# Weight halves, earlier casts, two stores on another queue, one difference moved: four small moves in a two-layer decoder trunk

## The chip, the cores and the metric

One core of one Trainium2 chip runs the whole program. It has five engines with a queue each: PE (matmuls), DVE (elementwise on vectors), ACT (activations and casts), POOL (GpSimd: masks, biases, and DMAs that add while they write) and SP (SyncE: it only issues DMAs). The engines run side by side, and each takes its own instructions strictly in the order of its queue. The metric is the time of one execution in device microseconds (us). The kernel before takes 1109.95 us, the median of three runs from 1109.84 to 1110.57.

## The reference, cut to what matters

The trunk has two layers over 512 positions of width 1024, in fp32. Layer 0 has a dilated attention with three groups of heads, layer 1 a forgetting attention with 16 heads of 64 on keys and values that are computed once; each is followed by a gated feed-forward net with a causal convolution.

```python
def fox_mixer(xn, w_q, w_o, k, v, c):
    q = (xn @ w_q).reshape(B, T, B_HEADS, HEAD_DIM)
    ...
        s = jnp.einsum('bqhd,bkhd->bhqk', q[:, q0:q1], k[:, :q1]) * scale
        s = s + (c_t[:, :, q0:q1, None] - c_t[:, :, None, :q1])
        s = jnp.where(causal, s, NEG)
        p = jax.nn.softmax(s, axis=-1)
        outs.append(jnp.einsum('bhqk,bkhd->bqhd', p, v[:, :q1]))
    ...
    return o.reshape(B, T, B_WIDTH) @ w_o

    # each layer: sandwich-normed mixer, then sandwich-normed feed-forward
    h = h + rms_norm(mix, g[1])
    f = conv_ffn(rms_norm(h, g[2]), w_up[l], conv_w[l], conv_b[l], w_down[l])
    h = h + rms_norm(f, g[3])
```

## The kernel before, in words

**Splitting.** Every fp32 operand of a large matmul is split into a high part (a cast to the shorter type fp32r, on ACT) and a low part (the original less the high part, on DVE). A product is then three matmuls on PE, one line each: high by high (L277), high by low (L278), low by high (L279). A weight of 128x1024 is loaded by SP into a buffer `wraw` (L49), cast by ACT (L57) and subtracted by DVE (L65). The class `W` keeps the order: `high` issues the next loads and the cast, `low` the subtraction. For the query weights of layer 1, `low_added` does the subtraction in a DMA instead: ACT writes the negated high part into the low part's place (L59), and a DMA of POOL adds `wraw` to it there (L82), so DVE has no part in it.

**Start.** Layer 0 begins with the projection of q and k (`qk_ps`). ACT and DVE norm a block of x (`sd`, `rs`, `xn`), PE transposes it (L345, `xt_ps`), ACT and DVE split the transposed block (L348, L349: `xah`, `xal`), and PE multiplies. The first weights come from `wearly`; those numbered 0, 1 and 2 are used by the first blocks, as soon as they are split.

**Forgetting attention.** It runs in steps m = 0 to 17; step m has a pair of heads j = m // 2 and two of the four blocks of queries (blocks 0 and 1 in even steps, 2 and 3 in odd ones). In a step stand, in this order: the scores (L1715, into four banks `s_ps`); the product of probabilities and values of step m-2 (L1762, into `o_ps`, from transposed probabilities `pT`); on DVE the score plus bias with its maximum (L1723), on ACT the exponential (L1725). Then, for each of the two blocks a = 0 and 1: the bias of step m+1 on POOL (L1696, with the causal mask L1697), a part of the next query projection (`q_ps`), the normalisation on DVE (L1733, L1735), the transposes of step m-1 on PE (L1747) and their copies on ACT (L1749); in late steps also a part of the output projection (`acc`) and the cast of an output weight. Every odd step ends with the high and low part of `o_ps` (L1772, L1776, `OTb`); every even step with the low part of the next queries (L1523, `qst`), which the scores two steps on multiply.

**Sums beside it.** Idle engines also prepare differences of blocks of the down projection's weights for the feed-forward net of layer 1. Loads bring them to `dsums`, DVE takes four differences of 128x512, and a store puts them into `dT` in memory, from where they are read much later. `down_sums` does this for two blocks (0 and 1) just ahead of the attention (`down1`; differences L607 to L610, two stores of 512 KB for each block, L615). `sums_between` does it for blocks 2 to 5 inside the attention: loads at the end of block a = 1 of step m = 2, 6, 10 and 14 (L1783 to L1785, on POOL), differences (L1787, L1788, L1790, L1791) in the two steps after it, then one store (L1793).

The order is written out by hand: generators are advanced by `next(...)` at given places. Buffers rotate in pools; `t4` holds biases, `ck` tiles (the rows of c of one pair of heads, loaded by SP, L1492) and `wraw` in turn, so a load can have to wait for the reader of an older tile.

Of the kernel before, what the change touches and what calls it, by code (L numbers as in the profile page):

```python
# [9 lines left out]
F32 = mybir.dt.float32  # L10
# [3 lines left out]
ALU = mybir.AluOpType  # L14
# [12 lines left out]

SEVEN = (5, 6, 8, 9, 11, 12, 14, 15, 17, 18)
ND = NF // 2
LAST = 3  # L30
FILL = 26


class Weights:
# [18 lines left out]
    def high(self, minus=False):  # L53
        if self.n_split < len(self.pieces):
            self.load(self.n_split + 1 + self.ahead_dma)
            raw, pair = self.raw.pop(self.n_split), self.new_pair()
            self.nc.scalar.copy(pair[:, 0], raw)  # L57
            if minus:
                self.nc.scalar.activation(pair[:, 1], raw, AF.Copy, scale=-1.0)  # L59
            self.half_done.append((raw, pair))  # L60

    def low(self):
        if self.half_done:
            raw, pair = self.half_done.pop()
            self.nc.vector.tensor_tensor(pair[:, 1], raw, pair[:, 0].bitcast(F32), ALU.subtract)  # L65
            if self.n_split in self.kept:
                self.kept[self.n_split] = raw
            self.ready[self.n_split] = (pair[:, 0], pair[:, 1])
            self.n_split += 1
# [32 lines left out]
def trunk_kernel(ctx, tc, x, norm_gains, w_qkv_a, w_o_a, w_q_b, w_o_b, kv_norm, w_kvf, b_f,  # L102
                 w_up, conv_w, conv_b, w_down, rope, out):
    nc = tc.nc
    act, dve, pool, pe, sp = nc.scalar, nc.vector, nc.gpsimd, nc.tensor, nc.sync
# [56 lines left out]

    dT = [tc.dram_tile([ND, 128, 2048], F32, name=f"dT{l}") for l in range(2)]

# [44 lines left out]
    W = Weights(nc, new_raw, lambda: t8([128, 2, 1024], F32R, name="w"), pieces)  # L209
# [382 lines left out]
    def down_sums(pairs, place, queue, lag, behind):  # L592


        live, n = [], len(pairs)
        for i in range(n + lag + behind):
            if i < n:
                l, j = pairs[i]
                a, b = place()
                live.append((a, b))  # L600
                r = w_down[l][j * 256:j * 256 + 256, :].rearrange("(c p) d -> c p d", p=128)
                sp.dma_start(a, r[0])
                sp.dma_start(b[:, 0:512], r[1, :, 512:1024])
                sp.dma_start(b[:, 512:1024], r[1, :, 0:512])
            if 0 <= i - lag < n:
                a, b = live[i - lag]
                dve.tensor_tensor(a[:, 0:512], a[:, 512:1024], a[:, 0:512], ALU.subtract)  # L607
                dve.tensor_tensor(a[:, 512:1024], b[:, 0:512], a[:, 512:1024], ALU.subtract)
                dve.tensor_tensor(b[:, 0:512], b[:, 0:512], a[:, 0:512], ALU.subtract)
                dve.tensor_tensor(b[:, 512:1024], b[:, 512:1024], b[:, 0:512], ALU.subtract)  # L610
            i -= lag + behind
            if i >= 0:
                l, j = pairs[i]
                for q, t in enumerate(live[i]):
                    queue.dma_start(dT[l][j, :, q * 1024:q * 1024 + 1024], t)  # L615
            yield

    def in_one():
# [13 lines left out]
    def ffn(l, bd, cp, nxt, ahead):  # L632
# [343 lines left out]
        for c in range(2, NF):  # L976
            if c == NF - 4:
                pair_load(0)
            if c == NF - 3:
                sums = down_sums([(l, ND - 1), (1, 8 + l)], in_one, pool, 1, 0)  # L980
                next(sums)
            if c in SEVEN:
                x21, x22 = [(xT[0][i], xT[1][i], s) for i, s in ((1, LO), (1, HI))]
# [311 lines left out]
    W.ahead = 4  # L1295
    W.split(6)
    qk_post(0, 3, qk_banks[3])
    sums = down_sums([(1, 6), (1, 7)], in_two, sp, 1, 3)
    next(sums)
    reorder(2, 3)  # L1300

# [23 lines left out]
        act.copy(V[1][:, b, :], o[:, 0:256])  # L1325
        dve.tensor_copy(V[2][:, b, :], o[:, 256:512])

    down0 = down_sums([(0, j) for j in range(10)], in_one, sp, 1, 1)
# [307 lines left out]
    for bp in range(2):  # L1636
        for s in range(2):
            t = slice(bp * 128, bp * 128 + 128)
# [13 lines left out]
                mm3(vc[bp], ah, al, w4[s][0][:, k, :], w4[s][1][:, k, :], False, False, True)  # L1652
        keep_values(0, bp, vc[bp])
    del w4
    down1 = down_sums([(1, j) for j in range(2)], in_two, pool, 1, 1)
    for c in range(4, 8):
        if c == 7:
            for i in range(4):
# [119 lines left out]
    def sums_between(l, j):  # L1778

        t = t8([128, 2, 1024], name="dsums")  # L1780
        a, b = t[:, 0], t[:, 1]
        r = w_down[l][j * 256:j * 256 + 256, :].rearrange("(c p) d -> c p d", p=128)
        pool.dma_start(a, r[0])  # L1783
# [3 lines left out]
        dve.tensor_tensor(a[:, 0:512], a[:, 512:1024], a[:, 0:512], ALU.subtract)  # L1787
        dve.tensor_tensor(a[:, 512:1024], b[:, 0:512], a[:, 512:1024], ALU.subtract)  # L1788
        yield
        dve.tensor_tensor(b[:, 0:512], b[:, 0:512], a[:, 0:512], ALU.subtract)  # L1790
# [18 lines left out]
    sums, idle = {}, itertools.repeat(None)  # L1809
    for j, m in ((2, 2), (3, 6), (4, 10), (5, 14)):  # L1810
        g = sums_between(1, j)
        for i in ((m, 1), (m + 1, 2), (m + 2, 0), (m + 2, 1)):
            sums[i] = g
    for m in range(M + 2):
        live = m < M
# [16 lines left out]
        for a in range(2):  # L1832
# [11 lines left out]
                f_transpose(pairs[m - 1][0], pairs[m - 1][1] + a)  # L1844
            if 0 <= 2 * m + a - FILL < len(fill):
                po.both(*fill[2 * m + a - FILL])
            if live and (j, i) >= (6, 2):
                W.low()
            if live and (j, i) >= (6, 1) and W.n_split < wo + 4:
                W.high()  # L1850
        if live and i0 == 0:
            q_low(j + 1)
# [56 lines left out]
```

## Time and profile before

| | |
|---|---|
| median of three runs | 1109.95 us (1109.84 to 1110.57) |
| profiled execution | 1110.27 us, of which the span of the trace is 1108.5 us |
| granted TensorE clock | 0.998 |
| PE busy | 1098.4 us, 99% of the span |
| DVE, ACT, POOL busy | 81%, 60%, 20% |
| DMA | 237.32 MB, 214 GB/s on average |

In the timeline a row has the start and the busy time in us, the engine, the line, the operation, the tile written and the tiles read, the shape, and the number of instructions merged; in brackets stands the time that the engine sat idle before it, and what ended that. The matmuls are pipelined: a 128x512 matmul shows 0.39 us, but the next starts 0.23 us after it, so for PE the distance from start to start is read. The attention of layer 1 lies between 615 and 724 us, step 5 begins at 648.93, step 13 at 700.29.

### The profile page before, as it was taken

To read this page: it belongs to the slowest core of one execution; us is meant where nothing else is said; L and a number is where in the kernel's file an instruction comes from. 1 tells how busy PE (TensorE), PEld (TensorE's weight loads), DVE (VectorE), ACT (ScalarE), POOL (GpSimd) and SP (SyncE) were. 2 spreads that over 40 slices of the span, in tenths; PEclk is the share of its full clock that TensorE was granted. 3 is DMA by queue.
4 is the path that set the end of the run, shared out by engine and by line. 5 is a ranking of instruction groups with operands and counts; after the bars stand their busy time and mean duration, and the time that the engine had idled before them with its cause. 6 is when DMAs were issued, how large, how long until landed. Compare 5 with 4: busy or idle time off the path is not lost.

```text
span 1108.5 us, 18139 instructions
## 1 busy us (share of the span) xinstructions
PE 1098.4 (99%) x6611; PEld 948.4 (86%) x6611; DVE 896.6 (81%) x1494; ACT 660.2 (60%) x1092; POOL 222.2 (20%) x329
## 2 busy tenths in 40 slices
PE   9999999999999999999999999999999999999997
PEld 6988889889999988888888787789989999988886
DVE  6577878978887799997877777858978887799995
ACT  5444566566565547476555677756565565547473
POOL 1832100211111111000010766600211111111000
PEclk9999999999999999999999999999999999999999
DMA  9469864467789989885872677584467779999872
GB/s 325 149 207 408 346 171 132 108 134 196 176 201 216 256 318 341 295 310 108 210 153 76 193 222 211 161 246 124 114 133 191 181 200 219 249 315 340 306 247 77
DMA packets 184563, 237.32 MB, mean 214 GB/s; under 512 B 11737, under 2 KB 131529, under 8 KB 183962
## 3 DMA queue, kind: packets, MB, share of 16 engines
q1 hardware_dynamic: 166970, 176.61, 49.0%
q0 software_dynamic: 17504, 59.55, 23.3%
q8 instruction: 52, 0.85, 0.3%
q14 instruction: 37, 0.30, 0.1%
HBM read 170.28 MB, written 39.63 MB: 189 GB/s over the span
## 4 chain that ended last, share of the span: by engine, by line
PE 89%; DVE 3%; issue 3%; ACT 2%; DMA 2%; POOL 1%; DVEq 0%; POOLq 0%; ACTq 0%
PE up L278 13%; PE up L277 13%; PE up L279 13%; PE acc L278 8%; PE acc L277 8%; PE acc L279 8%; PE qk_ps L278 2%; PE qk_ps L277 2%; PE qk_ps L279 2%; PE first L279 1%; PE first L277 1%; PE first L278 1%; PE o_ps L1762 1%; PE pT_ps L1747 1%; PE v_ps L278 1%
## 5 line engine op out<-in xcount | busy, mean ns | idle before, releaser
L277 PE MATMUL acc<-w 128*128 128x512 f32 (+1 forms) x311 | 120.5, 388 | 0.0
L279 PE MATMUL acc<-w 128*128 128x512 f32 (+1 forms) x311 | 120.4, 387 | 0.0
L57 ACT CAST w<-wraw 128x1024 fp32r<-128x1024 f32 x96 | 99.0, 1048 | 9.5 <-issue 3.9
L278 PE MATMUL acc<-w 128*128 128x512 f32 (+1 forms) x267 | 103.2, 387 | 0.0
L65 DVE TENSOR_TENSOR w<-wraw,w 128x1024 fp32r<-128x1024 f32 x66 | 88.1, 1356 | 15.1 <-ACT w L57 14.7
L641 ACT ACTIVATE bb<-up,conv 128x512 f32<-128x512 f32 x80 | 60.0, 776 | 67.3 <-DVE up L1022 42.8
L278 PE MATMUL up<-xbl,w 128*128 128x512 f32 (+1 forms) x280 | 96.3, 344 | 0.0
L278 PE MATMUL up<-xcl,w 128*128 128x512 f32 (+1 forms) x280 | 96.3, 344 | 0.0
L277 PE MATMUL up<-xch,w 128*128 128x512 f32 (+1 forms) x280 | 96.3, 344 | 0.0
L277 PE MATMUL up<-xbh,w 128*128 128x512 f32 (+1 forms) x280 | 96.3, 344 | 0.0
L279 PE MATMUL up<-xbh,w 128*128 128x512 f32 (+1 forms) x280 | 96.2, 344 | 0.0
L279 PE MATMUL up<-xch,w 128*128 128x512 f32 (+1 forms) x280 | 96.2, 344 | 0.0
L277 PE MATMUL up<-xsh,w 128*128 128x256 f32 x320 | 90.6, 283 | 0.0
L278 PE MATMUL up<-xsl,w 128*128 128x256 f32 x320 | 90.6, 283 | 0.0
L279 PE MATMUL up<-xsh,w 128*128 128x256 f32 x320 | 90.6, 283 | 0.0
L277 PEld LDWEIGHTS acc<-w 128*128 128x128 f32 x311 | 58.4, 188 | 12.0
L279 PEld LDWEIGHTS acc<-w 128*128 128x128 f32 x311 | 58.4, 188 | 11.8
L644 DVE SCALAR_TENSOR_TENSOR bb<-up,conv,bb 128x510 f32<-128x510 f32 x80 | 59.9, 749 | 2.8
L642 DVE SCALAR_TENSOR_TENSOR bb<-up,conv,bb 128x511 f32<-128x511 f32 x80 | 59.4, 742 | 2.6 <-ACT bb L641 2.6
L277 PEld LDWEIGHTS up<-xsh,w 128*128 128x128 f32 x320 | 61.4, 192 | 0.0
L278 PEld LDWEIGHTS up<-xsl,w 128*128 128x128 f32 x320 | 61.4, 192 | 0.0
L279 PEld LDWEIGHTS up<-xsh,w 128*128 128x128 f32 x320 | 61.4, 192 | 0.0
(337 smaller groups left out, 3161.2 us busy)
## 6 DMA issues: line engine op xcount, KB each, us to landing
wraw<-in_w_up_dram SPq DMA_DIRECT2D x88, 512.0 KB, 5.0
w<-wraw POOLq DMA_DIRECT2D x50, 512.0 KB, 6.1
dT<-dsums SPq DMA_DIRECT2D x24, 512.0 KB, 6.0
hD<-hc POOLq DMA_DIRECT2D x44, 256.0 KB, 7.6
dact<-hD SPq DMA_DIRECT2D x44, 256.0 KB, 5.2
wraw<-dT SPq DMA_DIRECT2D x22, 512.0 KB, 6.6
wraw<-in_w_down_dram SPq DMA_DIRECT2D x22, 512.0 KB
dsums<-in_w_down_dram SPq DMA_DIRECT2D x18, 512.0 KB, 5.6
```

The costliest lines, as they stand in the source:

```text
L57: self.nc.scalar.copy(pair[:, 0], raw)
L65: self.nc.vector.tensor_tensor(pair[:, 1], raw, pair[:, 0].bitcast(F32), ALU.subtract)
L277: pe.matmul(o, ah, bh, start=first, stop=False, skip_group_check=shared)
L278: pe.matmul(o, ah, bl, start=False, stop=False, skip_group_check=shared)
L279: pe.matmul(o, al, bh, start=False, stop=last, skip_group_check=shared)
L641: act.activation(bb[:, s, :], ps, AF.Identity, bias=cp[:, 3, ch:ch + 1], scale=cp[:, 2, ch:ch + 1])
L642: dve.scalar_tensor_tensor(bb[:, s, 1:], ps[:, :T - 1], cp[:, 1, ch:ch + 1], bb[:, s, 1:], ALU.mult, ALU.add)
L644: dve.scalar_tensor_tensor(bb[:, s, 2:], ps[:, :T - 2], cp[:, 0, ch:ch + 1], bb[:, s, 2:], ALU.mult, ALU.add)
L1747: pe.transpose(o[:, k0 + k, :], p[:, hh, k * 128:(k + 1) * 128], ident)
L1762: pe.matmul(o[64 * hh:64 * hh + 64, i * 128:(i + 1) * 128], Vt[hd // 8][:, k, (hd % 8) * 64:(hd % 8) * 64 + 64], pT[j, i, hh][:, k, :], st ...
```

## The change

Four edits, none of which changes what is computed or the order on PE.

First, the weights numbered 1 and 2 of the first projection are cast and subtracted in two halves of 512 columns, each an instruction of its own, so that PE can wait for a half. Second, the stores of block 1 of `down1` are issued by SP and no longer by POOL; those of block 0 stay on POOL. Third, `sums_between` stops once more, and its first difference moves ahead: from the end of step m+1 to the middle of it, before the normalisation of the second block. Fourth, the output weights 1 to 3 are cast half a step sooner, from (head pair 6, block 0) on instead of block 1, and subtracted half a step sooner, from block 1 on instead of block 2.

```diff
+HALVES = [(slice(0, 1024),), (slice(0, 512), slice(512, 1024))]
...
             raw, pair = self.raw.pop(self.n_split), self.new_pair()
-            self.nc.scalar.copy(pair[:, 0], raw)
+            for s in HALVES[self.n_split in (1, 2)]:
+                self.nc.scalar.copy(pair[:, 0, s], raw[:, s])
...
             raw, pair = self.half_done.pop()
-            self.nc.vector.tensor_tensor(pair[:, 1], raw, pair[:, 0].bitcast(F32), ALU.subtract)
+            for s in HALVES[self.n_split in (1, 2)]:
+                self.nc.vector.tensor_tensor(pair[:, 1, s], raw[:, s], pair[:, 0, s].bitcast(F32), ALU.subtract)
...
                 for q, t in enumerate(live[i]):
-                    queue.dma_start(dT[l][j, :, q * 1024:q * 1024 + 1024], t)
+                    queue[min(i, len(queue) - 1)].dma_start(dT[l][j, :, q * 1024:q * 1024 + 1024], t)
...
-    down1 = down_sums([(1, j) for j in range(2)], in_two, pool, 1, 1)
+    down1 = down_sums([(1, j) for j in range(2)], in_two, [pool, sp], 1, 1)
...
         dve.tensor_tensor(a[:, 0:512], a[:, 512:1024], a[:, 0:512], ALU.subtract)
+        yield
         dve.tensor_tensor(a[:, 512:1024], b[:, 0:512], a[:, 512:1024], ALU.subtract)
...
-        for i in ((m, 1), (m + 1, 2), (m + 2, 0), (m + 2, 1)):
+        for i in ((m, 1), (m + 1, 1), (m + 1, 2), (m + 2, 0), (m + 2, 1)):
             sums[i] = g
...
-            if live and (j, i) >= (6, 2):
+            if live and (j, i) >= (6, 1):
                 W.low()
-            if live and (j, i) >= (6, 1) and W.n_split < wo + 4:
+            if live and (j, i) >= (6, 0) and W.n_split < wo + 4:
                 W.high()
```

The other calls of `down_sums` only put their queue into a list. Line numbers of the kernel after are higher by one to four (L615 is L618 there, L82 is L85).

POOL's queue at the start of the attention, before: biases and masks of head pair 0, with the stores of block 1 in the middle, then the adding DMA.

```order
130 L1696 TENSOR_SCALAR bias<-ck,cq 128x256 x2
131 L1697 AFFINE_SELECT bias<-bias 128x2x128
132 L615 DMA dT_76<-dsums 128x1024 x2
133 L1696 TENSOR_SCALAR bias<-ck,cq 128x384 x2
134 L1697 AFFINE_SELECT bias<-bias 128x2x128
135 L1696 TENSOR_SCALAR bias<-ck,cq 128x512 x2
136 L1697 AFFINE_SELECT bias<-bias 128x2x128
137 L82 DMA w<-wraw 128x1024
```

SP's queue at the same place, after:

```order
208 L50 DMA wraw<-in_w_q_b_dram 128x8x128
209 L1495 DMA ck<-cd 128x1024
210 L618 DMA dT_76<-dsums 128x1024 x2
211 L1495 DMA ck<-cd 128x1024
212 L50 DMA wraw<-in_w_q_b_dram 128x8x128
213 L1495 DMA ck<-cd 128x1024
```

The two stores have left POOL's row 132 and stand on SP between the first and the second load of ck, which stood side by side before.

DVE's queue at the end of steps 3, 7, 11 and 15, the end of step 7 as an example, before (`ISA` is the maximum of the next step's first block):

```order
830 L1735 TENSOR_SCALAR bias<-bias,rl 128x384 x2
831 L1733 RECIPROCAL rl<-ls 128x2
832 L1735 TENSOR_SCALAR bias<-bias,rl 128x512 x2
833 L1776 TENSOR_TENSOR OTb_6797<-o_ps,OTb_6797 128x512
834 L1787 TENSOR_TENSOR dsums<-dsums 128x512
835 L1788 TENSOR_TENSOR dsums<-dsums 128x512
836 L1723 ISA bias,nm<-s_ps,bias 128x128
```

And after:

```order
830 L1738 TENSOR_SCALAR bias<-bias,rl 128x384 x2
831 L1790 TENSOR_TENSOR dsums<-dsums 128x512
832 L1736 RECIPROCAL rl<-ls 128x2
833 L1738 TENSOR_SCALAR bias<-bias,rl 128x512 x2
834 L1779 TENSOR_TENSOR OTb_6801<-o_ps,OTb_6801 128x512
835 L1792 TENSOR_TENSOR dsums<-dsums 128x512
836 L1726 ISA bias,nm<-s_ps,bias 128x128
```

One of the two differences now stands ahead of a reciprocal, whose input ACT delivers.

ACT's queue in steps 12 and 13, before (`pT` are copies of transposed probabilities, `w<-wraw` casts of output weights):

```order
457 L1749 COPY pT<-pT_ps 128x384 x2
458 L1749 COPY pT<-pT_ps 128x512 x2
459 L57 CAST w<-wraw 128x1024
460 L1725 ACTIVATE bias,ls<-bias,nm 128x384 x2
461 L1725 ACTIVATE bias,ls<-bias,nm 128x512 x2
462 L1772 CAST OTb_7188<-o_ps 128x512
463 L1749 COPY pT<-pT_ps 128x256
464 L57 CAST w<-wraw 128x1024
465 L1749 COPY pT<-pT_ps 128x512
466 L57 CAST w<-wraw 128x1024
```

And after:

```order
457 L1752 COPY pT<-pT_ps 128x384 x2
458 L59 CAST w<-wraw 128x1024
459 L1752 COPY pT<-pT_ps 128x512 x2
460 L59 CAST w<-wraw 128x1024
461 L1728 ACTIVATE bias,ls<-bias,nm 128x384 x2
462 L1728 ACTIVATE bias,ls<-bias,nm 128x512 x2
463 L1775 CAST OTb_7192<-o_ps 128x512
464 L1752 COPY pT<-pT_ps 128x256
465 L59 CAST w<-wraw 128x1024
466 L1752 COPY pT<-pT_ps 128x512
```

Each of the three casts moved up by a place; on DVE the subtractions moved likewise, the first from behind the maxima of step 13 to ahead of them.

More of the change, by code (lines that the diff above doesn't have):

```diff
@@ L979, in ffn @@
             if c == NF - 3:
-                sums = down_sums([(l, ND - 1), (1, 8 + l)], in_one, pool, 1, 0)
+                sums = down_sums([(l, ND - 1), (1, 8 + l)], in_one, [pool], 1, 0)
                 next(sums)
@@ L1297, in trunk_kernel @@
     qk_post(0, 3, qk_banks[3])
-    sums = down_sums([(1, 6), (1, 7)], in_two, sp, 1, 3)
+    sums = down_sums([(1, 6), (1, 7)], in_two, [sp], 1, 3)
     next(sums)
@@ L1326, in v_post @@
         dve.tensor_copy(V[2][:, b, :], o[:, 256:512])
-    down0 = down_sums([(0, j) for j in range(10)], in_one, sp, 1, 1)
+    down0 = down_sums([(0, j) for j in range(10)], in_one, [sp], 1, 1)
     v_proj0([[L(qk_transpose, 0, 0), L(qk_transpose, 0, 1)],
```

## The prediction

> **What bounds the kernel now.** I read the page's busy times first, then the waits of PE, then the timeline round each wait.
>
> ```profile
> PE 1098.4 (99%) x6611; PEld 948.4 (86%) x6611; DVE 896.6 (81%) x1494; ACT 660.2 (60%) x1092; POOL 222.2 (20%) x329
> ```
>
> PE is busy for 1098.4 of 1108.5 us, and the change takes no matmul away. So it can only gain where PE stands still, and lose where it makes PE stand still anew. The list of PE's waits, with the line, the releaser, the total, the number and the longest, says where:
>
> ```profile
> PE qk_ps L278 <- DVE w L65: 1.0, 2, 0.8
> PE q_ps L279 <- DMA w<-wraw: 0.8, 1, 0.8
> PE acc L278 <- DVE w L65: 0.8, 1, 0.8
> ```
>
> These are four idle times. A restart costs a little more than the idle time, so below I count from start to start. A fifth place, scores that run slowly, shows only in the timeline.
>
> **A. The halved weights.** The timeline at the start, the idle time and its releaser in brackets:
>
> ```profile
> 12.54 1.41 DVE L296 SCALAR_TENSOR_TENSOR xn<-h,rs,gain 128x512 f32<-128x512 f32 x2
> ...
> 13.86 1.22 DVE L65 TENSOR_TENSOR w<-wearly,w 128x1024 fp32r<-128x1024 f32 x1
> 14.16 1.12 ACT L348 CAST xah<-xt_ps 128x512 fp32r<-128x512 f32 x2 [0.91 <-PE xt_ps L345]
> 14.41 0.47 PE L277 MATMUL qk_ps<-w,xah 128*128 128x512 f32 x1
> 15.00 1.28 DVE L349 TENSOR_TENSOR xal<-xt_ps,xah 128x512 fp32r<-128x512 f32 x2
> 15.48 0.40 PE L279 MATMUL qk_ps<-w,xal 128*128 128x512 f32 x1
> ...
> 21.32 0.48 PE L277 MATMUL qk_ps<-w,xah 128*128 128x512 f32 x1
> 21.87 0.39 PE L279 MATMUL qk_ps<-w,xal 128*128 128x512 f32 x1
> ```
>
> The first wait, at 12.2, will go, and gain nothing. PE would reach the eight transposes (L345) about 1 us sooner, but the last four need the second half of xn, which DVE ends at 13.95 (12.54 + 1.41). So the wait only moves there. The second is real: from L277 to L279 PE took 1.07 us (14.41 to 15.48), against 0.55 undisturbed (21.32 to 21.87). The first half of the low part would be there at 13.86 + 0.64 (half of the pair of 1.28) = 14.50, before PE wants it at about 14.7. That gains 0.52. Against it stand the added instructions: two casts of 512 columns take 1.12 (row 14.16, from PSUM, the nearest) where one of 1024 takes 1.05, and two subtractions 1.28 for 1.22, so xn and all behind it come about 0.1 later. Two values of w share this; net 0.42, between 0.3 and 0.52. I take 0.4.
>
> The Trainium skill speaks against splitting: its page "VectorE: DVE Perf Modes" (section on the TRN2 errata) says that VectorE and ScalarE pay a fixed latency for each instruction that reads SBUF, some 224 cycles on ScalarE. By it a halved cast would cost 0.19 more, an estimate from that figure at 1.2 GHz, and A would be 0.3. The rows above say 0.07, from PSUM; no run so far shows the SBUF form.
>
> **B. Two stores from POOL to SP.** The timeline round the third wait:
>
> ```profile
> 612.10 3.38 SPq L1492 DMA_DIRECT2D ck<-cd  x2
> 618.80 0.78 DVE L610 TENSOR_TENSOR dsums<-dsums 128x512 f32<-128x512 f32 x1
> 622.01 1.12 POOL L615 DMA_DIRECT2D dT<-dsums  x2
> 624.90 1.05 ACT L59 ACTIVATE w<-wraw 128x1024 fp32r<-128x1024 f32 x1
> 626.26 0.41 POOL L1697 TENSOR_SCALAR_AFFINE_SELECT bias<-bias 128x256 f32<-128x256 f32 x1
> 627.59 0.94 POOL L82 DMA_DIRECT2D w<-wraw  x1 [0.93 <-ACT bias L1725]
> ...
> 632.77 0.39 PE L278 MATMUL q_ps<-xql,w 128*128 128x512 f32 x1
> 633.99 0.50 PE L279 MATMUL q_ps<-xqh,w 128*128 128x512 f32 x1 [0.83 <-DMA w<-wraw]
> ...
> 638.93 0.90 POOL L82 DMA_DIRECT2D w<-wraw  x1 [1.41 <-ACT w L59]
> ```
>
> PE waits for a weight that POOL's accumulating DMA (L82) completes. That DMA stands behind the masks of the first head pair, and these behind the two stores, 1.12 us of POOL. Without them the last mask ends near 625.5 instead of 626.67; ACT's negated weight is there at 625.95. The DMA can then start at about 626.3, at 0.3 after ACT or 0.9 after the mask alike, and 1.25 sooner than 627.59. It took 6.4 us to PE's restart, so the weight is there at 632.7, and PE wants it at 632.77 + 0.23 = 633.0. The whole slip, 633.99 - 633.0 = 0.99, goes; I take 1.0, and 0 to 1.0 as bounds. The lower one is because the 0.93 of idle time ahead of L82 is put down to ACT's exponentials (L1725), which L82 has no use for; were something at a fixed time behind it, nothing would be gained.
>
> On SP the stores wait for DVE's differences, the last of which ends at 619.58, and behind them stands the load of the second ck, issued by 615.48 before (612.10 + 3.38) and now near 620. POOL's first bias of the second head pair, right behind L82, needs it at about 627, seven us later. A load of ck takes 4.5 (below), so I cost that at nothing; a rival prices it.
>
> ```profile
> ck<-cd SPq DMA_DIRECT2D x5, 512.0 KB, 4.5
> ```
>
> **C. The first difference moved forward.** A step's scores are 12 matmuls (L1715). Rows of PE in steps 5, 7 and 9, of DVE in steps 3 to 8, and POOL's first load of the sums of step 2 with its time to landing:
>
> ```profile
> 648.93 2.00 PE L1715 MATMUL s_ps<-kst,qst 64*128 64x384 f32 x12
> ...
> 662.37 1.49 PE L1715 MATMUL s_ps<-kst,qst 64*128 64x384 f32 x12
> ...
> 675.31 1.98 PE L1715 MATMUL s_ps<-kst,qst 64*128 64x384 f32 x12
> ...
> 640.05 0.85 DVE L1735 TENSOR_SCALAR bias<-bias,rl 128x384 f32<-128x384 f32 x2
> ...
> 643.10 0.86 DVE L1787 TENSOR_TENSOR dsums<-dsums 128x512 f32<-128x512 f32 x1
> ...
> 649.23 0.68 DVE L1523 TENSOR_TENSOR qst<-q_ps,qst 128x512 fp32r<-128x512 f32 x1
> ...
> 667.71 0.17 DVE L1733 RECIPROCAL rl<-ls 128x2 f32<-128x2 f32 x1 [0.36 <-ACT bias L1725]
> ...
> 672.41 1.12 DVE L1790 TENSOR_TENSOR dsums<-dsums 128x512 f32<-128x512 f32 x1
> ...
> 635.84 0.58 POOL L1783 DMA_DIRECT2D dsums<-in_w_down_dram  x1
> ```
>
> ```profile
> dsums<-in_w_down_dram POOLq DMA_DIRECT2D x1, 512.0 KB, 5.7
> ```
>
> Steps 5 and 9 take 2.00 and 1.98, step 7 takes 1.49: 0.5 lost twice. In step 5 the scores begin at 648.93, and the low part of the queries (L1523) that their last bank needs ends at 649.91, behind four differences on DVE. The moved difference (0.86) fills DVE's idle 0.36 ahead of the reciprocal of step 7, and I see no other gap on DVE from there to step 9, so the low part comes 0.4 to 0.5 sooner there and step 9's 0.5 goes. In step 3 the difference may stand too early: its load, issued at 635.84, lands 5.7 later, at 641.5, when DVE is ready for it at 640.9 (640.05 + 0.85). DVE then waits 0.6 with the normalisation behind it, which leaves 0.2 of the gain for step 5, or takes as much if the load is half a us later. Together 0.7, between 0.2 and 1.0.
>
> The Trainium skill, "SBUF — State Buffer", section "Who interferes with whom", says that a DVE instruction with two SBUF inputs contends with a GpSimd instruction that reads SBUF. The moved difference then meets POOL's biases. The trace bears this out: the same 128x512 difference took 0.86 and 1.12 in the rows above. With 1.12 at the new place C would be 0.3 less, 0.4.
>
> **D. Output weights half a step sooner.** The timeline round the last wait:
>
> ```profile
> 700.28 1.82 ACT L1749 COPY pT<-pT_ps 128x384 f32<-128x384 f32 x4
> ...
> 700.29 1.83 PE L1715 MATMUL s_ps<-kst,qst 64*128 64x384 f32 x12
> 701.97 1.07 ACT L57 CAST w<-wraw 128x1024 fp32r<-128x1024 f32 x1
> 705.73 1.22 DVE L65 TENSOR_TENSOR w<-wraw,w 128x1024 fp32r<-128x1024 f32 x1
> 705.76 0.47 PE L277 MATMUL acc<-w,OTb 128*128 128x512 f32 x1
> 707.00 0.50 PE L278 MATMUL acc<-w,OTb 128*128 128x512 f32 x1 [0.77 <-DVE w L65]
> 707.59 0.59 ACT L1749 COPY pT<-pT_ps 128x512 f32<-128x512 f32 x1
> 709.28 0.88 PE L1762 MATMUL o_ps<-pT,Vt 128*64 128x128 f32 x12
> ```
>
> The low part moves from 705.73 to about 701.7, long ahead of its use at 705.99: the slip of 707.00 - 705.76 - 0.23 = 1.01 goes. The price is on ACT and DVE. The cast (1.07) now stands between the copies of 384 and of 512 columns, so PE's second half of L1762 in step 13 waits some 0.2 for the last copy; but these copies themselves come 0.5 sooner by C, which frees the banks that the scores of step 13 waited for (1.83 against 1.49 in step 7: 0.35). The subtraction (1.22) stands ahead of the maxima of step 13; 0.5 of it is paid by C, so they come 0.7 later, and with them the copy at 707.59, which then ends at 708.9. PE, 1.2 earlier, wants it at 708.3 for L1762 (709.28 + 0.25 - 1.2): 0.55 are given back there as a new wait. Net 1.0 + 0.35 - 0.2 - 0.55 = 0.6, between 0 and 1.35. I take it that step 14, which loses its subtraction, makes up the rest of the delay.
>
> **The sum.** 0.4 + 1.0 + 0.7 + 0.6 = 2.7 us. The profiled execution took 1110.27 us (span 1108.5 and 1.8 around it), 0.3 above the median of the three runs, 1109.95. It should come to 1107.6, its span to 1105.8, the median to 1107.3.
>
> **The rivals.** First, L82's start is tied to something else, or the DMA takes longer: B is 0, and the median 1108.3. For it speaks the 0.93 without a reason, against it the next row of L82, which starts 0.3 after ACT's last write. Second, ACT and DVE give back what C and D win: the copies of step 13 and 14 and the wait for the load in step 3 eat 1.3, and the median is 1108.6; for it speaks that both engines have no gap in those steps. Third, the better end: the new waits stay away, C is 1.0 and D 1.35, and the median 1106.2. Fourth, on the other side, slower: the second ck, behind the two stores on SP, lands too late. If nothing hides it, every us by which it lands after 627 is a us of POOL, then of DVE and PE. To lose the 2.7 and 2.2 more it must land at 632, 12 us after its issue. Its like took 4.5, so little speaks for it; the time would be 1112.2.
>
> **How the numbers follow.** About 0.2%, 2.2 us, is what a measurement can tell from no change here. My forecast has 0.60, of which 0.47 lie beyond 2.2 us; the first rival 0.13, the second 0.12, both within 0.2%; the third 0.07; the fourth, with any other stall that I overlooked, 0.08. So faster 0.54, same 0.38, slower 0.08. The range runs from 1105.8 (the third case and 0.4 for the spread between runs) to 1109.6 (A and a little of C alone).
>
> **What would show it.** In the profile after: no wait of qk_ps near 14.7, and the one at 12.2 replaced by one ahead of the transposes; L82 issued near 626 and no wait of q_ps; 1.4 us of scores in step 9; no wait of acc for w; a new short wait of L1762 on ACT's copies near 708. I am wrong if L82 still starts at 627.6, if DVE stands waiting for the sums' load in step 3 for over half a us, or if the wait on ACT's copies is as long as the one removed.

## The result, and the profile after

The kernel after took 1107.07 us (median of nine executions, 1106.76 to 1108.18), the kernel before 1110.21 on the same chip (1109.84 to 1110.57). The ratio is 0.9974, with a 95% interval of 0.9964 to 0.9983: faster, by 3.1 us. The forecast was 1107.3.

The page's busy times of the kernel after, and then its list of PE's waits (total, number, longest):

```profile
PE 1096.4 (99%) x6611; PEld 948.4 (86%) x6611; DVE 897.6 (81%) x1496; ACT 660.1 (60%) x1094; POOL 222.8 (20%) x327
```

```profile
PE o_ps L1765 <- ACT pT L1752: 0.6, 1, 0.6
PE xt_ps L348 <- DVE xn L299: 0.4, 1, 0.4
PE qk_ps L280 <- ACT xah L351: 0.2, 1, 0.2
PE v_ps L280 <- ACT vp L1417: 0.2, 1, 0.2
```

The waits for weights are gone (the 0.2 of `v_ps` is for another tile), and two have come in their places: the transposes of the start, and the product of probabilities and values of step 14 (L1765), in its second half. Both were forecast, the second one shorter than it is.

To see where the time went, I compare matmul with matmul. All 6611 stand in the same order in every kernel here, so each has a start in the one trace and in the other; the difference, before less after, is PE's lead. It changes only where PE waits more or less. The lead of the profiled execution after over that before, at the times of before:

| stretch, us of before | what changes there | lead gained | forecast |
|---|---|---|---|
| 0 to 14 | first loads, and the cost of splitting (A) | 0.12 | -0.1 |
| 14 to 16 | low half of the second weight (A) | 0.54 | 0.5 |
| 16 to 570 | scattered, none over 0.1 | 0.14 | 0 |
| 570 to 584 | a wait of `v_ps` | 0.48 | 0 |
| 631 to 640 | the weight that POOL's DMA completes (B) | 1.11 | 1.0 |
| 645 to 655 | scores of step 5 (C) | 0.42 | 0.2 |
| 668 to 680 | scores of step 9 (C) | 0.34 | 0.5 |
| 700 to 703 | scores of step 13 (C), then its product L1765 (D) | 0.24 | 0.35 and -0.2 |
| 703 to 708 | wait of `acc` (D) | 1.04 | 1.0 |
| 708 to 711 | new wait of `o_ps` in step 14 (D) | -0.81 | -0.55 |
| 711 to 716 | transposes of step 14 (D) | -0.29 | 0 |
| 716 to the end | | 0.04 | 0 |

Together 3.37. The forecast's 0.4 for A stands in two rows, its gain of 0.52 and its cost of 0.1, because the cost falls before 14 us.

**A.** The timeline of the start, on PE, ACT and DVE:

```profile
13.22 1.31 PE L348 MATMUL xt_ps<-ident,xn 128*128 128x128 f32 x8 [0.43 <-DVE xn L299]
14.29 0.48 PE L280 MATMUL qk_ps<-w,xah 128*128 128x512 f32 x1
...
14.83 0.39 PE L282 MATMUL qk_ps<-w,xal 128*128 128x512 f32 x1
...
12.09 1.12 ACT L59 CAST w<-wearly 128x512 fp32r<-128x512 f32 x2
...
13.74 1.29 DVE L68 TENSOR_TENSOR w<-wearly,w 128x512 fp32r<-128x512 f32 x2
```

From L280 to L282 PE now takes 0.54 (14.29 to 14.83), against 1.07 before. The two half casts of this weight take 1.12, where one of 1024 columns takes 1.05; the two subtractions 1.29, against 1.22. For the weight numbered 1 the halves take 1.15 and 1.29. So splitting costs 0.07 to 0.10 on ACT and 0.06 to 0.07 on DVE. By the prediction's estimate from the Trainium skill, "VectorE: DVE Perf Modes" (section on the TRN2 errata), the halved cast would have been 0.19 dearer; for this SBUF form the trace does not agree.

**B.** SP and POOL where the attention starts, and PE at the fourth product of the query weight:

```profile
616.73 1.91 SPq L618 DMA_DIRECT2D dT<-dsums  x2
618.74 0.38 SPq L1495 DMA_DIRECT2D ck<-cd  x1
...
623.76 0.41 POOL L1700 TENSOR_SCALAR_AFFINE_SELECT bias<-bias 128x256 f32<-128x256 f32 x1
624.97 0.90 POOL L85 DMA_DIRECT2D w<-wraw  x1 [0.80 <-ACT w L61]
...
630.78 1.48 POOL L1699 TENSOR_SCALAR bias<-ck,cq 128x512 f32<-128x512 f32 x2 [0.23 <-DMA w<-wraw]
...
631.72 0.39 PE L282 MATMUL q_ps<-xqh,w 128*128 128x512 f32 x1
```

L85 is issued at 624.97, which with PE's lead of 1.28 is 626.25 in the times of before; forecast were 626.3. POOL itself waits for the same DMA and goes on at 630.78, so it is there 5.8 us after its issue, and PE's L282, at 631.72, needs no wait. The second load of `ck`, at 618.74 behind the two stores, holds up nothing: no row of POOL waits for it.

**C.** DVE in steps 3 to 5, PE's scores of steps 5 and 9, and POOL's first load of the sums:

```profile
638.44 0.88 DVE L1790 TENSOR_TENSOR dsums<-dsums 128x512 f32<-128x512 f32 x1
...
642.97 1.12 DVE L1794 TENSOR_TENSOR dsums<-dsums 128x512 f32<-128x512 f32 x1
644.12 1.06 DVE L1795 TENSOR_TENSOR dsums<-dsums 128x512 f32<-128x512 f32 x1
...
646.42 0.68 DVE L1526 TENSOR_TENSOR qst<-q_ps,qst 128x512 fp32r<-128x512 f32 x1
...
646.54 1.58 PE L1718 MATMUL s_ps<-kst,qst 64*128 64x384 f32 x12
...
672.50 1.64 PE L1718 MATMUL s_ps<-kst,qst 64*128 64x384 f32 x12
...
632.68 0.58 POOL L1786 DMA_DIRECT2D dsums<-in_w_down_dram  x1
```

The scores of step 5 take 1.58 where they took 2.00, those of step 9 1.64 where they took 1.98; 1.49 is undisturbed. The moved difference starts at 638.44 without any wait for its load.

**D.** PE, ACT and DVE in steps 13 and 14:

```profile
702.38 0.48 PE L280 MATMUL acc<-w,OTb 128*128 128x512 f32 x1
702.69 0.39 PE L281 MATMUL acc<-w,OTb 128*128 128x512 f32 x1
...
704.84 0.44 PE L1765 MATMUL o_ps<-pT,Vt 128*64 128x128 f32 x4
705.88 0.66 PE L1765 MATMUL o_ps<-pT,Vt 128*64 128x128 f32 x8 [0.60 <-ACT pT L1752]
...
708.57 1.32 PE L1750 MATMUL pT_ps<-ident,bias 128*128 128x128 f32 x8
...
704.30 1.06 ACT L59 CAST w<-wraw 128x1024 fp32r<-128x1024 f32 x1
705.25 0.58 ACT L1752 COPY pT<-pT_ps 128x512 f32<-128x512 f32 x1
...
706.34 1.41 DVE L68 TENSOR_TENSOR w<-wraw,w 128x1024 fp32r<-128x1024 f32 x1
707.67 0.68 DVE L1779 TENSOR_TENSOR OTb<-o_ps,OTb 128x512 fp32r<-128x512 f32 x1
```

PE passes L281 of `acc` without a wait. In step 14 it begins L1765 at 704.84 and then stands for the copy that ACT begins only at 705.25, behind the cast. The eight transposes of step 14 take 1.32, against 1.04 in the kernel before. A cast stood ahead of that copy before, too; what has changed is when ACT's chain begins. The first exponential of step 13, before and after:

```profile
703.28 0.62 ACT L1725 ACTIVATE bias<-bias,nm 128x384 f32<-128x384 f32 x1 [0.24 <-DVE nm L1723]
```

```profile
700.94 0.62 ACT L1728 ACTIVATE bias<-bias,nm 128x384 f32<-128x384 f32 x1 [0.71 <-DVE nm L1726]
```

It waits for DVE's maxima. Step 13 begins at 700.29 before and at 697.14 after, so it comes 2.99 behind the first score before, and 3.80 after: 0.81 later. The copy begins 7.30 and 8.11 behind it, later by the same 0.81.

### The profile page after: what moved, and what is told of

The parts are those of the page before. It is cut to its first block, busy times and chain, and to the rows that moved or that the text cites. A ratio compares the mean times of both kernels' runs of the same rounds, so it can differ in the third digit from the quotient of the medians.

```text
span 1105.0 us, 18142 instructions
## 1 busy us (share of the span) xinstructions
PE 1096.4 (99%) x6611; PEld 948.4 (86%) x6611; DVE 897.6 (81%) x1496; ACT 660.1 (60%) x1094; POOL 222.8 (20%) x327
## 4 chain that ended last, share of the span: by engine, by line
PE 96%; ACT 2%; DVE 1%; issue 0%; DVEq 0%; ACTq 0%
PE up L280 13%; PE up L281 13%; PE up L282 13%; PE acc L280 8%; PE acc L282 8%; PE acc L281 8%; PE v_ps L280 2%; PE v_ps L281 2%; PE v_ps L282 2%; PE qk_ps L280 2%; PE qk_ps L282 2%; PE qk_ps L281 2%; PE o_ps L1765 2%; PE q_ps L280 2%; PE pT_ps L1750 1%; PE s_ps L1718 1%
## 5 line engine op out<-in xcount | busy, mean ns | idle before, releaser
L280 PE MATMUL acc<-w 128*128 128x512 f32 (+1 forms) x311 | 120.5, 388 | 0.0
L282 PE MATMUL acc<-w 128*128 128x512 f32 (+1 forms) x311 | 120.4, 387 | 0.0
L281 PE MATMUL acc<-w 128*128 128x512 f32 (+1 forms) x267 | 103.2, 387 | 0.0
L281 PE MATMUL up<-xbl,w 128*128 128x512 f32 (+1 forms) x280 | 96.3, 344 | 0.0
L281 PE MATMUL up<-xcl,w 128*128 128x512 f32 (+1 forms) x280 | 96.3, 344 | 0.0
L280 PE MATMUL up<-xbh,w 128*128 128x512 f32 (+1 forms) x280 | 96.3, 344 | 0.0
L280 PE MATMUL up<-xch,w 128*128 128x512 f32 (+1 forms) x280 | 96.3, 344 | 0.0
L282 PE MATMUL up<-xbh,w 128*128 128x512 f32 (+1 forms) x280 | 96.2, 344 | 0.0
L282 PE MATMUL up<-xch,w 128*128 128x512 f32 (+1 forms) x280 | 96.2, 344 | 0.0
L280 PE MATMUL up<-xsh,w 128*128 128x256 f32 x320 | 90.6, 283 | 0.0
L281 PE MATMUL up<-xsl,w 128*128 128x256 f32 x320 | 90.6, 283 | 0.0
L282 PE MATMUL up<-xsh,w 128*128 128x256 f32 x320 | 90.6, 283 | 0.0
L280 PEld LDWEIGHTS acc<-w 128*128 128x128 f32 x311 | 58.4, 188 | 11.9
L282 PEld LDWEIGHTS acc<-w 128*128 128x128 f32 x311 | 58.4, 188 | 11.9
L280 PEld LDWEIGHTS up<-xsh,w 128*128 128x128 f32 x320 | 61.4, 192 | 0.0
L281 PEld LDWEIGHTS up<-xsl,w 128*128 128x128 f32 x320 | 61.4, 192 | 0.0
L282 PEld LDWEIGHTS up<-xsh,w 128*128 128x128 f32 x320 | 61.4, 192 | 0.0
```

The source lines that it names most:

```text
L280: pe.matmul(o, ah, bh, start=first, stop=False, skip_group_check=shared)
L281: pe.matmul(o, ah, bl, start=False, stop=False, skip_group_check=shared)
L282: pe.matmul(o, al, bh, start=False, stop=last, skip_group_check=shared)
```

## The experiments

In the first four runs each edit is made alone on the kernel before; they ran on one chip, where the kernel before took 1110.65. The next four are built on the kernel after and ran on another, where before took 1110.42.

**A alone.**

```diff
-            self.nc.scalar.copy(pair[:, 0], raw)
+            for s in HALVES[self.n_split in (1, 2)]:
+                self.nc.scalar.copy(pair[:, 0, s], raw[:, s])
...
-            self.nc.vector.tensor_tensor(pair[:, 1], raw, pair[:, 0].bitcast(F32), ALU.subtract)
+            for s in HALVES[self.n_split in (1, 2)]:
+                self.nc.vector.tensor_tensor(pair[:, 1, s], raw[:, s], pair[:, 0, s].bitcast(F32), ALU.subtract)
```

> Only the two weights in halves. PE's lead is how much earlier a matmul starts than its like in the kernel before. My theory: the lead is 0.6 us after the second weight (near 15 us) and stays; the wait of v_ps near 582 us, which is far from this edit, stays as it was; about 1109.6 us. Rival: the start of the program also sets off what is seen later, and the v_ps wait of 0.2 us and the small drift up to 580 us go with this edit alone, which gives a lead of 1.2 us at 600 us and about 1109.0.

1109.33 us, ratio 0.9988 (0.9979 to 0.9998). The lead grows by 0.54 from 14 to 16 us, the size of the kernel after, and by 0.46 between 570 and 584: the `v_ps` wait goes with this edit alone, as the rival had it, though none of the edit lies near 580 us.

**B alone.**

```diff
-                    queue.dma_start(dT[l][j, :, q * 1024:q * 1024 + 1024], t)
+                    queue[min(i, len(queue) - 1)].dma_start(dT[l][j, :, q * 1024:q * 1024 + 1024], t)
...
-    down1 = down_sums([(1, j) for j in range(2)], in_two, pool, 1, 1)
+    down1 = down_sums([(1, j) for j in range(2)], in_two, [pool, sp], 1, 1)
```

> Only the two stores on SP. My theory: POOL's adding DMA starts 0.3 us after ACT's negated weight and the lead grows by 1.1 us at the wait of q_ps, nothing else moves; about 1109.1 us. Rival: the loads of ck behind the stores come late and POOL or DVE waits for them in the second head pair, which takes half a us or more of the 1.1 away.

1109.52 us, ratio 0.9993 (0.9983 to 1.0002): the interval takes in 1, so the time alone does not show a gain. In the profiled execution the lead grows by 1.11 at 631 to 640 us, the 1.0 forecast; but this execution had lost 0.88 in its first 14 us, in code that the edit does not touch, and ends only 0.06 ahead. ACT's negated weight, POOL's last mask and the DMA:

```profile
625.96 1.06 ACT L59 ACTIVATE w<-wraw 128x1024 fp32r<-128x1024 f32 x1
...
626.12 0.41 POOL L1697 TENSOR_SCALAR_AFFINE_SELECT bias<-bias 128x256 f32<-128x256 f32 x1
627.32 0.91 POOL L82 DMA_DIRECT2D w<-wraw  x1 [0.79 <-DMA wraw<-in_w_q_b_dram]
```

L82 starts 0.30 after ACT's end at 627.02, the same as in the kernel after (624.97, ACT's end at 624.67). The mask ends 0.8 ahead of it in both, so these two traces alone do not part the two; the later rows of L82 do, which start 0.30 after ACT and 3.8 us or more after the mask before them. The gain at this place is 1.10 or 1.11 in all eight traces with both stores on SP.

**C alone.**

```diff
         dve.tensor_tensor(a[:, 0:512], a[:, 512:1024], a[:, 0:512], ALU.subtract)
+        yield
         dve.tensor_tensor(a[:, 512:1024], b[:, 0:512], a[:, 512:1024], ALU.subtract)
...
-        for i in ((m, 1), (m + 1, 2), (m + 2, 0), (m + 2, 1)):
+        for i in ((m, 1), (m + 1, 1), (m + 1, 2), (m + 2, 0), (m + 2, 1)):
```

> Only the first difference moved. My theory, as predicted: without the stores' edit the loads of step 2 land too late for the difference in step 3, DVE waits some 0.6 us there, and step 5 gains 0.2 us or less, step 9 0.4 and step 13 0.2 to 0.3: a lead of 0.8, about 1109.4 us. Rival: the load is there in time without it, step 5 gains 0.4 as in the full change, and the lead is 1.0.

1109.82 us, ratio 0.9996 (0.9986 to 1.0005): again the time alone shows no gain. The lead grows by 0.08 in step 5, 0.33 in step 9 and 0.34 in step 13. DVE in step 3:

```profile
641.75 0.74 DVE L1787 TENSOR_TENSOR dsums<-dsums 128x512 f32<-128x512 f32 x1 [0.53 <-DMA dsums<-in_w_down_dram]
```

This is the wait for the load that the prediction put at 0.6. In the kernel after it is missing because of B: POOL, rid of the two stores, issues that load at 632.68 and no longer at 635.84, 3.2 us sooner, while PE is only 2.4 ahead. C is worth 0.3 more in step 5 beside B than alone.

**D alone.**

```diff
-            if live and (j, i) >= (6, 2):
+            if live and (j, i) >= (6, 1):
                 W.low()
-            if live and (j, i) >= (6, 1) and W.n_split < wo + 4:
+            if live and (j, i) >= (6, 0) and W.n_split < wo + 4:
```

> Only the casts and subtractions of output weights half a step sooner. My theory: DVE is the bound in steps 12 to 14; the wait for w goes (1.05), but without the 0.5 us that the moved difference saves on DVE all that follows is 1.2 us late instead of 0.7, so the new waits take 1.2 and more and the edit alone gains nothing or loses up to 0.5 us: 1110.2 to 1110.7. Rival: the edit is worth the 0.6 us of the prediction by itself, 1109.6.

1111.37 us, ratio 1.0007 (0.9998 to 1.0016): no gain. The lead loses 0.02 in the scores of step 13 and 0.38 in its product (L1762, which has the copies of 512 columns behind the cast now), gains 1.05 at `acc`, and loses 0.55 at `o_ps` and 0.32 in the rest of step 14: -0.22 together. Without C beside it, this edit pays a little more than it wins.

**The kernel after again, on the chip of the next runs.**

> The changed kernel once more, beside the three below on the same chip: about 1107.1 us, and PE's lead over the kernel before grows at the same places as in its first profile, within 0.1 us at each, while the lead in the first 15 us may differ by up to a us, as it did between the single edits.

1107.17 us, ratio 0.9970 (0.9959 to 0.9982). From 16 us on the lead grows by the same steps; at 16 us it is 0.37 where it was 0.66, and 2.97 at the end. What differs is the first 14 us, which no edit changes but A.

**After without D.**

```diff
-            if live and (j, i) >= (6, 1):
+            if live and (j, i) >= (6, 2):
                 W.low()
-            if live and (j, i) >= (6, 0) and W.n_split < wo + 4:
+            if live and (j, i) >= (6, 1) and W.n_split < wo + 4:
```

> The changed kernel without the fourth edit, so the casts and subtractions of the output weights stand where they stood before. My theory: the fourth edit nets about 0.2 us in the full change (1.05 + 0.24 won, 0.81 and 0.29 given back), so this kernel takes the same time to 0.2 us, about 1107.3; the wait of acc for w is back with a slip of 1.0, and the waits for the copies and before the transposes of step 14 are gone. The prediction's figure would be 0.6 us slower than the changed kernel, 1107.7.

1107.30 us, ratio 0.9971 (0.9959 to 0.9982), beside 1107.17 for the kernel after. Two rows of PE, in steps 13 and 14:

```profile
703.95 0.50 PE L281 MATMUL acc<-w,OTb 128*128 128x512 f32 x1 [0.77 <-DVE w L68]
...
706.21 0.88 PE L1765 MATMUL o_ps<-pT,Vt 128*64 128x128 f32 x12
```

The wait of `acc` is back and that of `o_ps` is gone: its twelve matmuls run through. From 700 to 716 us the lead grows by 0.33 without D (0.35 of it in the scores of step 13) and by 0.18 with D. So D wins nothing in the kernel after, and the quicker scores of step 13 are C's.

**After, with the third cast behind ACT's copy of 512 columns.**

```diff
+            if live and (j, i) == (6, 3):
+                W.high()
             if live and (j, i) >= (6, 1):
                 W.low()
-            if live and (j, i) >= (6, 0) and W.n_split < wo + 4:
+            if live and (j, i) in ((6, 0), (6, 1)):
                 W.high()
```

> The changed kernel with the last of the three casts behind the copy of 512 columns in step 13 and no longer ahead of it. My theory: ACT's order is only the last link and DVE is the bound in steps 12 to 14; the wait of o_ps for the copy (0.8) goes, and the transposes of step 14 wait that much longer for DVE's maxima, so the time is that of the changed kernel to 0.2 us. Rival: the cast ahead of the copy is the cause, and 0.8 us are won: 1106.3.

1107.59 us, ratio 0.9976 (0.9966 to 0.9986). PE in steps 13 and 14:

```profile
704.82 0.88 PE L1765 MATMUL o_ps<-pT,Vt 128*64 128x128 f32 x12
...
708.41 0.66 PE L1750 MATMUL pT_ps<-ident,bias 128*128 128x128 f32 x4 [0.54 <-DVE OTb L1779]
709.27 0.63 PE L1750 MATMUL pT_ps<-ident,bias 128*128 128x128 f32 x4 [0.19 <-DVE nm L1726]
```

The wait on ACT is gone, and two on DVE come some 3 us later. What ACT gave back, DVE took: DVE is the bound there, and ACT's cast stood only in front of it.

**After, with DVE relieved:** the last two differences of the sums of step 10 move from step 12 to step 14.

```diff
-        for i in ((m, 1), (m + 1, 1), (m + 1, 2), (m + 2, 0), (m + 2, 1)):
+        last = ((14, 2), (15, 0)) if m == 10 else ((m + 2, 0), (m + 2, 1))
+        for i in ((m, 1), (m + 1, 1), (m + 1, 2), *last):
```

> The changed kernel with the last two differences of the sums of step 10 at the end of step 14, where DVE stands idle, and no longer in step 12. That takes 2.2 us of DVE from the front of the queue in steps 12 and 13. My theory, that DVE is the bound there: both new waits (0.8 of o_ps, 0.3 before the transposes) go, and 1.1 us are won, about 1106.0. Rival: ACT's casts ahead of the copies hold PE, and less than 0.3 is won.

1106.91 us, ratio 0.9970 (0.9958 to 0.9981). Between 703 and 716 us the lead grows by 0.43, against -0.06 in the kernel after: about half of what was expected. PE in step 14, and DVE in step 12:

```profile
706.06 0.66 PE L1765 MATMUL o_ps<-pT,Vt 128*64 128x128 f32 x8 [0.36 <-ACT pT L1752]
...
698.78 1.23 DVE L68 TENSOR_TENSOR w<-wraw,w 128x1024 fp32r<-128x1024 f32 x1 [1.07 <-ACT w L59]
```

DVE, with two differences less, now stands 1.07 us for ACT's cast. The bound has gone to ACT.

**Before, with one of the two stores on SP**, to see what held L82 back.

```diff
-    down1 = down_sums([(1, j) for j in range(2)], in_two, pool, 1, 1)
+    down1 = down_sums([(1, j) for j in range(2)], in_two, [pool, pool, sp], 1, 1)
```

The store's queue is chosen there by `min(i + q, ...)`, so that only the second store of block 1 goes to SP.

> The kernel before with only the second of the two stores on SP, so POOL still issues one (0.56 us), and its last mask ends at about 626.1, just after ACT's negated weight (625.95). In the kernel before the adding DMA started 0.93 after the mask and 1.64 after ACT, with both stores on SP 0.3 after ACT. Theory one: a DMA of POOL that adds starts some 0.8 to 0.9 after the last instruction of POOL, and at 627.0 here; the wait of q_ps shrinks by 0.55. Theory two: it starts 0.3 after ACT or right after the mask, and something else held it up before; it starts near 626.3 and nearly all of the wait is gone.

One execution: 1111.19 us, beside 1109.93 for the kernel before. ACT, POOL and PE:

```profile
625.27 1.06 ACT L59 ACTIVATE w<-wraw 128x1024 fp32r<-128x1024 f32 x1
...
626.16 0.41 POOL L1697 TENSOR_SCALAR_AFFINE_SELECT bias<-bias 128x256 f32<-128x256 f32 x1
626.68 0.91 POOL L82 DMA_DIRECT2D w<-wraw  x1
...
634.83 0.50 PE L279 MATMUL q_ps<-xqh,w 128*128 128x512 f32 x1 [1.24 <-DMA w<-wraw]
```

L82 follows ACT by 0.35 and the mask by 0.11, so it needs no 0.9 behind a mask. It is issued 0.91 sooner than before, and nothing comes of it: PE restarts 8.15 us later (626.68 to 634.83), not 6.4. So neither theory held whole: the start was the second one's, the wait stayed. The store that stayed on POOL was in flight until 630.07, 7.7 us after its issue. POOL's DMA queue moved 0.52 MB from 626.5 to 629.3 us, the size of the store, and 0.53 MB from 629.3 to 634, that of the adding DMA; in the kernel before it had moved both stores (1.05 MB) by 627 and then nothing until 629. By these sizes the adding DMA's bytes came behind the store's. Why the store moved so late was not followed.

**Before, with weight 2 alone in halves.**

```diff
-            for s in HALVES[self.n_split in (1, 2)]:
+            for s in HALVES[self.n_split == 2]:
```

(in both places of A)

> The kernel before with only the weight numbered 2 in halves. As predicted, halving the weight numbered 1 only moves a wait, so this gains what both halves gain from 11 us to 16 us (0.6 in both profiles with the first edit). Rival: with the weight 1 whole, the norm and the subtraction of weight 2 come later on DVE, and less than 0.4 is won.

One execution: 1109.46 us, beside 1109.93. The lead grows by 0.54 from 14 to 16 us and by 0.48 from 570 to 584, all that A has. The first wait stays as it was, and its halving is worth nothing:

```profile
PE qk_ps L281 <- DVE w L68: 0.8, 1, 0.8
```

**Each cast half a step sooner still**, so that step 13 has none on ACT and one subtraction less on DVE; once on the kernel after with DVE relieved, once on the kernel after itself, side by side on a third chip (before 1110.38).

```diff
-            if live and (j, i) >= (6, 1):
+            if live and (j, i) >= (6, 0):
                 W.low()
-            if live and (j, i) >= (6, 0) and W.n_split < wo + 4:
+            if live and (j, i) >= (5, 3) and W.n_split < wo + 4:
```

With DVE relieved:

> Nothing of the computation is changed. As the run before it (the last two differences of the sums of step 10 moved to step 14), and besides each of the three output weights is cast and subtracted half a step sooner still: the first cast at the end of step 11, where ACT then waits 1.27 us for DVE's maxima, and no cast is left in step 13, one subtraction instead of two on DVE there. Theory, the wait of o_ps in step 13 (0.36 idle, 0.57 from start to start) is the cast ahead of the copy of 512 columns: that copy then starts near 704.5 instead of 705.43, no wait of o_ps is left, and about 0.6 more is won: 1106.3. Rival, DVE is as full in step 12 as in step 13, and the subtraction that is moved into its first half (1.2 us between two reciprocals) makes the normalisation late: a new wait of pT_ps or of the scores in step 12 of 0.5 or more, and 1106.9 or above.

1106.57 us, ratio 0.9967 (0.9955 to 0.9980). ACT's copy in step 13 no longer has a cast ahead of it, and PE runs through:

```profile
705.10 0.88 PE L1765 MATMUL o_ps<-pT,Vt 128*64 128x128 f32 x12
...
704.01 0.85 ACT L1752 COPY pT<-pT_ps 128x256 f32<-128x256 f32 x2
```

With the differences left in step 12:

> Nothing of the computation is changed. As the kernel after, and each of the three output weights cast and subtracted half a step sooner still, so that step 13 has no cast on ACT and one subtraction less on DVE, but keeps the two differences of sums. Theory, both new waits of the kernel after (o_ps 0.81, pT_ps 0.29 from start to start) are this cast and this subtraction: both go, 1.0 is won: 1106.1. Rival, DVE is the bound of step 13 through the differences: the o_ps wait goes, the pT_ps wait grows, half of it or less is won: 1106.6 or above. If step 12 pays, as in the rival of the run beside it, nothing is won: 1107.1.

1107.62 us, ratio 0.9978 (0.9969 to 0.9986). PE and DVE in steps 12 and 13:

```profile
705.78 1.14 PE L1765 MATMUL o_ps<-pT,Vt 128*64 128x128 f32 x12 [0.30 <-ACT pT L1752]
...
699.90 1.21 DVE L68 TENSOR_TENSOR w<-wraw,w 128x1024 fp32r<-128x1024 f32 x1
```

The second subtraction of step 12 begins at 699.90, 1.3 later than its like in the kernel beside it (698.56), and the low part of the queries (from 701.03) and the maxima of step 13 stand behind it. So step 12 pays, and nothing is won. The lead from 703 to 716 us in all of these:

| kernel | lead gained, 703 to 716 us |
|---|---|
| after without D | -0.02 |
| after | -0.06 |
| third cast behind the copy | -0.10 |
| casts sooner still | -0.08 |
| DVE relieved | 0.43 |
| DVE relieved and casts sooner still | 0.82 |

Moving ACT's work alone wins nothing, relieving DVE wins half, and both together win the whole wait of `o_ps`; about 0.2 of the loss at the transposes stays. The last kernel has the lowest median of all. It ran on another chip than the kernel after, and its interval overlaps that kernel's, so the times alone do not part the two. In the traces PE gains 3.59 from 16 us to the end in it, and 2.71 in the kernel after.

## Why the prediction was right, and where it was not

The time and the sign came out as forecast, and so did A and B. C came out by two errors that cancel, D paid nothing, and a gain that no term had made up for it: in these parts the agreement is luck.

**A** was right: the first wait only moved to the transposes, and the second gained 0.54 gross for 0.52. The cost of 0.1 is only hinted at: with the second weight alone in halves the lead at 16 us is 0.54, with both weights it is 0.37 in A alone and in the repeat of the kernel after, but the first 14 us vary by more than that. What the prediction did not have is the 0.48 at `v_ps`. It listed the three places of waits for weights and left out the small one. Every kernel with the second weight in halves gains about 0.46 there, and the four others lose 0.2 to 0.3 against the one trace of the kernel before. The traces carry it back as far as a load, for which ACT waits before a cast of another weight, some 16 us ahead of that wait. Before, and with A alone:

```profile
566.76 1.05 ACT L1536 CAST w<-wraw 128x1024 fp32r<-128x1024 f32 x1 [2.18 <-DMA wraw<-in_w_kvf_dram]
```

```profile
565.58 1.05 ACT L1539 CAST w<-wraw 128x1024 fp32r<-128x1024 f32 x1 [1.48 <-DMA wraw<-in_w_kvf_dram]
```

This wait is 1.41 to 1.61 in all nine traces with the second weight in halves, and 2.18 to 2.48 in the five without. What ACT and DVE do from there to 577 us runs 0.92 to 1.18 ahead in A alone, where PE is 0.47 ahead. Why an edit at 14 us makes this wait shorter was not found.

**B** was right to a tenth: 1.11 for 1.0, the issue at 626.25 for 626.3, the DMA 5.8 for 6.4. The first rival, L82 tied to something else, fell with B alone. The fourth, the second `ck` too late behind the stores, fell too. Why L82 in the kernel before started 0.92 behind the mask is still open. It did so, by 0.92 to 0.94, in all five traces with both stores on POOL, and with one store there it did not, so the delay goes with the pair of stores; what ties it to them was not followed.

**C** was the right mechanism with the places mixed up. Step 9 gained 0.34 for 0.5. In step 5 the term "DVE then waits 0.6" was right for C alone (0.53), and wrong beside B, which brings the load forward: 0.42 for 0.2. Together that is 0.76 for 0.7. The 0.35 of step 13, which the prediction counted under D and put down to C, is C's: C alone gains it, and so does the kernel after without D; D alone does not. The weighing of the Trainium skill, "SBUF — State Buffer" ("Who interferes with whom"), came out between the two rows at the new place: the moved difference took 0.88, nearer to 0.86 than to 1.12.

**D** failed: 0.6 forecast. Its places hold 0.18 in the kernel after, of which C brings 0.35, so that the pair with and without the edit gives -0.15 of lead, and no difference in time that can be told. The gain at `acc` was right, 1.04 for 1.0, and so was the chain of the new wait at `o_ps`, from the subtraction over DVE's maxima to ACT's copy. Two terms had the wrong size. The "0.55 given back" was 0.81. C was to pay 0.5 of the delay of the maxima; the first exponential of step 13 came 0.30 sooner with C alone, 1.18 later with D alone and 0.81 later with both, for 0.7. And "step 14, which loses its subtraction, makes up the rest of the delay" was wrong: the transposes of step 14 lose 0.29. With the third cast behind the copy the trace shows what they wait for, the low part of `OTb` and the maxima on DVE, and DVE's delay there is larger and not smaller. In the kernel after the low part of `OTb` (L1779) starts 10.53 behind the first score of step 13, where before it started 8.98 behind it. Two instructions ahead of it on DVE had grown, the normalisation of 512 columns from 1.16 to 1.48 and the subtraction from 1.21 to 1.41; why was not tried. The 0.2 for the second half of L1762 in step 13 was 0.12 (0.38 with D alone).

The prediction's sign of being wrong, a wait on ACT's copies as long as the one removed, comes out so: 0.81 alone is shorter than 1.04, and with the other two losses it is longer. The second rival, that ACT and DVE give back what C and D win, was right about D and wrong about C. Its reason, no gap on either engine in those steps, is what the five runs that vary steps 12 to 14 show, with DVE as the first of the two.

By the prediction's own terms the 3.37 are 0.66 for A with the first 14 us (0.4), 0.48 at `v_ps` (nothing), 1.11 for B (1.0), 0.76 for C (0.7), 0.18 for D (0.6) and 0.18 elsewhere.

## What to carry to other kernels

When PE waits for a step on one engine and the work is moved earlier, ask which engine has room in the place it is moved to. Here two engines were full in the same two steps, and only moving work off both removed the whole wait. A chain of small edits should be priced as it stands together: freeing POOL made a load earlier, and with it another edit worth more. Read the lead of the bounding engine step by step; an end-to-end time of the four edits together would not have told that one of them paid nothing.

## What the runs showed of the hardware

Two differences of 128x512 on DVE took 1.12 and 1.06 us beside POOL's biases, and two of the same shape 0.68 and 0.69 where POOL stood idle. First POOL beside them in step 4 of the kernel after (the rows of DVE are shown above), then DVE and POOL in the kernel with the two of step 12 moved to step 14; in step 12 of the kernel after these had taken 1.12 and 1.06, too:

```profile
642.86 1.79 POOL L1699 TENSOR_SCALAR bias<-ck,cq 128x512 f32<-128x512 f32 x2
```

```profile
711.22 0.68 DVE L1794 TENSOR_TENSOR dsums<-dsums 128x512 f32<-128x512 f32 x1
711.94 0.69 DVE L1795 TENSOR_TENSOR dsums<-dsums 128x512 f32<-128x512 f32 x1
...
712.93 0.54 POOL L1797 DMA_DIRECT2D dT<-dsums  x1 [5.04 <-DVE dsums L1795]
```

So the place of such an instruction is worth 0.8 us for two; the Trainium skill's rule of the two engines that contend, in "SBUF — State Buffer" ("Who interferes with whom"), agrees. Whether POOL's reads are the whole reason was not tried. The runs with DVE relieved have both effects in them, the move and the shorter instructions.

The first 14 us differ from execution to execution: PE's lead at 14 us was between -0.88 and 0.35 over the profiled executions, in kernels whose start is the same too (-0.88, -0.09 and -0.09 with B, C and D alone). That is as much as one of these edits is worth, so a single execution cannot price them.

The DMA that adds while it writes took 5.8, 6.4 and 8.15 us from issue to PE's or POOL's restart for the same 512 KB. In the longest, POOL's DMA queue moved the 512 KB of a store first, from 626.5 to 629.3 us, though the adding DMA had been issued at 626.68.
